# Loading the weights of a two-layer MoE trunk: 2 MB double pages, w_down by whole rows, three loads in flight

## The chip, the core and the metric

The kernel runs on one core of a Trainium2 chip. The metric is the time of one execution in microseconds (us) on the device. Engines: PE (matrix multiply), DVE (VectorE), ACT (ScalarE), POOL (GpSimd) and SP (SyncE, which here only issues transfers), and 16 DMA engines that move data between the main memory and the core's on-chip memory.

## What is computed

Two layers work on 512 tokens of width 1024 in fp32. Each layer has an input projection, a token mixer (a gated MLP in layer 0, a short convolution in layer 1), cross-attention to 256 memory rows, an output projection, a layer norm, and then 16 experts, of which each token uses two:

```python
for i in range(DEPTH):
    z = x @ w_in                       # 1024 x 1536 or 1024 x 2048
    tok, q = ...                       # token mixer; queries
    xa = memory_cross_attention(q, mem, w_kv[i])
    o = jnp.concatenate([tok, xa], axis=-1) @ w_out[i]
    x = layer_norm(ALPHA * x + o, ln1_g[i], ln1_b[i])
    # router: one of 4 groups, two experts in it
    for e in range(N_EXPERTS):         # 16
        h = jax.nn.silu(xt @ w_gate[e]) * (xt @ w_up[e])     # 1024 x 512 each
        out = out + combine[:, e:e + 1] * (h @ w_down[e])    # 512 x 1024
    x = layer_norm(ALPHA * x + f, ln2_g[i], ln2_b[i])
```

An expert's three matrices have 2 MB each. All weights together have 222 MB, of which the experts have 192, and each is used once.

## The kernel before, in words

**Arithmetic.** An fp32 product is made of three matmuls (`mm3`, L172 to 176): a number is split into a high part of reduced precision and a low part, the rest. A weight therefore passes two engines before PE: ACT copies `raw` to `high` (L144), DVE computes `low = raw - high` (L145). The three matmuls stand on L174 (high, high), L175 (low) and L176.

**Pages.** The on-chip memory is cut into 24 pages of 8 KB per partition, 1 MB each (`page`, `drop`, L64 to 74). Everything large lives in them: activations, raw weights, split weights. A page that is dropped goes to the end of a list; the next tile takes the first one of the list and must wait until the last reader of that page is done. All of this is decided when the program is built.

**The weight stream.** `Stream` (L96) has the weights in the order of their use, in units of 1 MB. `pump` splits what is loaded, up to `ahead` halves in front of PE (4, and 6 among the experts, where `whole` splits a page at once), and loads the next unit when more pages are free than `keep` and what the splits still want (L155). `fetch` (L118) issues a load on SP's queue; a load waits until the one `flight` places before it has landed: 2 at the start, 4 among the experts.

```python
            elif len(self.todo) > self.stop and len(free_pages) > self.keep + max(0, self.ahead - len(self.ready)):
                self.fetch()
```

Gate and up matrices are loaded by pairs of rows (`add_pairs`), a contiguous 4 KB per partition and row block. `w_down` and the projections are loaded by column halves (`add`), in runs of 2 KB. `moe_weights` (L906) orders the units of an expert: gate and up of rows 0 to 511, gate and up of rows 512 to 1023, then the two column halves of the expert before.

**The experts.** `experts` (L622) goes over 16 experts. POOL gathers up to 128 tokens of an expert, PE transposes them (`xtrans`), multiplies by gate and up (`gate_up`, accumulators `ga`, `ua`), ACT and DVE form `h`, PE transposes it (`htrans`, tile `ht`, one buffer). One expert later `down` (L674) multiplies by `w_down`, one column half after the other (accumulator `ya`), ACT scales each half on its way out (L686), and POOL adds the rows to `rd` in the main memory by a scatter. Near the end `W.keep` and `W.stop` (L710) hold loads back so that pages stay free for the rest of the layer; a last sum (`ra`) and the second layer norm follow.

**Order.** A scheduler in the build orders the instructions of each engine by a simulated timeline; on the chip each engine runs its list in that order. Before each layer's experts stands a branch on `nover` (L853, for experts with more than 128 tokens, not taken here), over which no instruction is moved. At the start, SP's queue holds `mem`, two loads of `w_kv`, `x`, and then, issued by `late_dma`, the router's weights and three loads for layer 0's gating unit (`sgu`, L251 to 256), ahead of the second two loads of `w_kv`.

Of the kernel before, what the change touches and what calls it, by code (L numbers as in the profile page):

```python
# [18 lines left out]
FT = mybir.dt.float32  # L19
# [8 lines left out]
P = 128  # L28
# [14 lines left out]
N_PAGES = 24  # L43
# [4 lines left out]
def trunk(ctx, tc, x, mem, w_in_a, sgu_ln_g, sgu_ln_b, sgu_w, sgu_b, w_in_b, conv_w, w_kv, w_out,  # L48
# [13 lines left out]
    uid = [0]  # L62

# [8 lines left out]
    def drop(*ts):  # L72
        for t in ts:
            free_pages.append(held.pop(id(t))[0])

# [19 lines left out]

    class Stream:  # L96
        def __init__(self):
            self.todo, self.raw, self.ready = [], [], []
# [4 lines left out]
        def add_pairs(self, w, k0):  # L103

            self.todo.append(bass.AP(tensor=w.tensor, offset=w.offset + k0 * 512,
                                     ap=[[2 * 512, P], [256 * 512, 2], [1, 2 * 512]]))

        def add_wide(self, w, k0):

            self.todo.append(bass.AP(tensor=w.tensor, offset=w.offset + k0 * D, ap=[[D, P], [P * D, 2], [1, D]]))  # L110

        def add(self, w, k0, n0):

            n = w.shape[1]
            self.todo.append(bass.AP(tensor=w.tensor, offset=w.offset + k0 * n + n0,
                                     ap=[[n, P], [P * n, 4], [1, 512]]))

        def fetch(self):  # L118
            self.sent += 1
            t = page("raw", [P, 4, 512])  # L120
            src = self.todo.pop(0)
            with ExitStack() if self.behind is None else tc.issue_after(self.behind):
                load = sp.dma_start(t if src.ap[-1][1] == 512 else t.rearrange("p (a b) n -> p a (b n)", a=2), src).ins
# [5 lines left out]
            self.raw.append([t, 0])  # L129

        def split(self):
            t, h = self.raw[0]
            if self.whole and not h:
                high, low = page("high", [P, 4, 512], FR), page("low", [P, 4, 512], FR)
                src = t
                self.ready += [Half(high[:, 0:2], low[:, 0:2]), Half(high[:, 2:4], low[:, 2:4], high, low)]
                self.raw[0][1] = 2
            else:
                g = page("split", [P, 2, 2, 512], FR)
                src, high, low = t[:, 2 * h:2 * h + 2], g[:, 0], g[:, 1]  # L140
                self.ready.append(Half(high, low, g))
                self.raw[0][1] += 1
# [4 lines left out]
            if self.raw[0][1] == 2:  # L147
                self.raw.pop(0)
                drop(t)

        def pump(self):
            while True:
                size = 2 if self.whole and self.raw and not self.raw[0][1] else 1
                if not self.hold and len(self.ready) + size <= self.ahead and self.raw and len(free_pages) >= size:
                    self.split()  # L155
                elif len(self.todo) > self.stop and len(free_pages) > self.keep + max(0, self.ahead - len(self.ready)):
                    self.fetch()
                else:
                    return
# [35 lines left out]

    def weights_kv(i):
        w = w_kv[i]
        for n in range(2):
            for k in range(2):
                W.add(w, k * 512, n * 512)  # L200

    def weights_cols(w, n):
        for k in range(2):
            W.add(w, k * 512, n * 512)

    def weights_out(i):
        w = w_out[i]
        for n in range(2):
            for k in (1, 0):
                W.add(w, k * 512, n * 512)  # L210
# [3 lines left out]
    W.fetch()  # L214
    W.fetch()
# [29 lines left out]
    def late_dma(dst, src):  # L245
        with tc.issue_after(xload.ins):
# [6 lines left out]
    sgu = page("sgu", [P, 4, H, P])  # L253
    sgw, sgb, sgt, cwr = sgu[:, 0], sgu[:, 1], sgu[:, 2], sgu[:12, 3, 0]
    late_dma(cwr, conv_w.rearrange("o t (b p) -> (o t b) p", p=P))
    cw = consts.tile([P, 3, 4], FT, name="cw")
    late_dma(sgw, bass.AP(tensor=sgu_w.tensor, offset=sgu_w.offset, ap=[[P, P], [P * P, H], [1, P]]))
    late_dma(sgb.rearrange("p h i -> p (h i)"),
                  bass.AP(tensor=sgu_b.tensor, offset=sgu_b.offset, ap=[[0, P], [1, H * P]]))

# [361 lines left out]
    def experts(i, lnp, fill, after, stop, fine=False):  # L622
# [72 lines left out]
        W.keep, W.flight = 5, 4  # L695
# [4 lines left out]
        for e in range(E):  # L700
# [205 lines left out]
    def moe_weights(i, first):  # L906
        def gu(e, k):
            W.add_pairs(w_gate[i, e], k * 512)
            W.add_pairs(w_up[i, e], k * 512)

        def dn(e):
            for n in range(2):
                W.add(w_down[i, e], 0, n * 512)
# [25 lines left out]
    W.keep = 8  # L939
# [9 lines left out]
    sg = page("sgln", [P, 2, MW])  # L949
    bcast_rows(sg[:, 0], sgu_ln_g[0])  # L950
    bcast_rows(sg[:, 1], sgu_ln_b[0])
# [9 lines left out]

    W.keep = 4
    a = project_t(xh, xl)
    qh, ql = page("qh", [P, H, S], FR), page("ql", [P, H, S], FR)
    for h in range(H):
        split_to(qh[:, h, :], ql[:, h, :], a[h])
    pr = softmax_scores(qh, ql, kt)
    drop(qh, ql, kt)
# [12 lines left out]
    W.keep = 5  # L981
# [18 lines left out]
    W.keep = 3  # L1000
# [79 lines left out]
    W.keep = 3  # L1080
# [37 lines left out]
```

## Time and profile before

| | |
|---|---|
| median of 3 runs | 1069.66 us (1065.61 to 1069.82) |
| the profiled execution | 1064.45 us, span of the profile 1062.8 us |
| PE busy | 989.5 us, 93% of the span |
| DVE busy, ACT busy | 779.6 us, 630.6 us |
| DMA | 273.31 MB, mean 257 GB/s |
| first transpose for the experts of layer 0, of layer 1 | 217.4 us, 730.1 us from the span's start |
| first of layer 0's last sums | 532.5 us |

The profile has the times of one execution. A busy time sums what an engine worked; for PE, whose matmuls overlap, it says little beyond whether there were gaps. The DMA share of a stretch is the mean busy share of the 16 DMA engines, near 1 (and slightly over, by overlap) when they are full. A wait names the engine that waited, the line that waited, and what released it.

### The profile page before, as it was taken

How to read it: one execution, taken by the hardware profiler on the slowest of the kernel's cores; microseconds unless marked ns; L12 is line 12 of the kernel's file. 1: busy time of each engine (PE TensorE's matmuls, PEld its weight loads, DVE VectorE, ACT ScalarE, POOL GpSimd, SP SyncE). 2: the span in 40 equal slices, each digit the busy share in tenths (PEclk: the TensorE clock that was granted, in tenths of full speed). 3: DMA queues.
4: the chain of work that ended last, by engine and by line, in shares of the span. 5: the costliest groups of instructions: out<-in, count | busy, mean ns of one | idle time of the engine just before them, and what ended most of it. 6: DMA issues, size and time to landing. Idle time of an engine off the chain costs nothing.

```text
span 1062.8 us, 12859 instructions
## 1 busy us (share of the span) xinstructions
PE 989.5 (93%) x4815; PEld 809.4 (76%) x4816; DVE 779.6 (73%) x880; ACT 630.6 (59%) x684; POOL 177.1 (17%) x115
## 2 busy tenths in 40 slices
PE   8999999789999988999999999987899999988995
PEld 6788889668888876777678887875788888866863
DVE  4648657869898677878794656575799898768875
ACT  4536524458888667668553524234778887667762
POOL 0000014312212202001100000223053212220113
PEclk9999999979999999999999999987899999999998
DMA  9713449459999999979671424491699999999833
GB/s 327 269 41 119 156 162 319 160 195 360 358 370 371 367 349 365 336 274 321 200 280 40 159 79 152 146 401 45 210 355 362 372 361 360 347 359 336 282 68 154
DMA packets 102220, 273.31 MB, mean 257 GB/s; under 512 B 10442, under 2 KB 10966, under 8 KB 102152
## 3 DMA queue, kind: packets, MB, share of 16 engines
q1 hardware_dynamic: 89480, 242.84, 62.9%
q0 software_dynamic: 11808, 26.97, 9.2%
q10 hardware_dynamic: 864, 2.62, 0.7%
q8 instruction: 39, 0.64, 0.2%
q14 instruction: 29, 0.24, 0.1%
HBM read 262.22 MB, written 26.21 MB: 271 GB/s over the span
## 4 chain that ended last, share of the span: by engine, by line
PE 61%; DVE 8%; ACT 4%; DMA 4%; issue 2%; DVEq 0%; ACTq 0%; POOLq 0%; SPq 0%
PE ua L175 5%; PE ua L176 5%; PE ya L175 5%; PE ya L174 5%; PE ua L174 5%; PE ya L176 5%; PE ga L175 5%; PE ga L174 4%; PE ga L176 4%; DVE low L145 4%; ACT high L144 3%; PE xt L648 2%; PE za L176 2%; PE za L174 2%; PE za L175 2%; DMA raw<-in_w_up_dram 2%
## 5 line engine op out<-in xcount | busy, mean ns | idle before, releaser
L145 DVE TENSOR_TENSOR low<-raw,high 128x2048 fp32r<-128x2048 f32 x189 | 428.7, 2288 | 78.8 <-ACT high L144 73.0
L144 ACT ACTIVATE high<-raw 128x2048 fp32r<-128x2048 f32 x189 | 357.9, 1914 | 54.5 <-PE ga L175 20.1
L175 PE MATMUL ua<-low,xgt 128*128 128x512 f32 x248 | 98.6, 397 | 16.7 <-DVE low L145 16.6
L144 ACT ACTIVATE split<-raw 128x1024 fp32r<-128x1024 f32 x66 | 68.5, 1058 | 76.7 <-PE za L176 26.1
L174 PE MATMUL ya<-high,ht 128*128 128x512 f32 x256 | 103.9, 407 | 2.5 <-ACT high L144 2.5
L176 PE MATMUL ya<-high,ht 128*128 128x512 f32 x256 | 101.5, 398 | 2.5 <-DVE ht L180 2.5
L175 PE MATMUL ya<-low,ht 128*128 128x512 f32 x256 | 102.6, 401 | 0.7 <-DVE low L145 0.7
L174 PE MATMUL ga<-high,xgt 128*128 128x512 f32 x248 | 98.9, 399 | 3.0 <-ACT high L144 3.0
L175 PE MATMUL ga<-low,xgt 128*128 128x512 f32 x248 | 98.7, 398 | 2.1 <-DVE low L145 1.9
L174 PE MATMUL ua<-high,xgt 128*128 128x512 f32 x248 | 98.1, 395 | 0.2
L176 PE MATMUL ga<-high,xgt 128*128 128x512 f32 x248 | 97.6, 393 | 0.0
L176 PE MATMUL ua<-high,xgt 128*128 128x512 f32 x248 | 97.0, 391 | 0.0
L145 DVE TENSOR_TENSOR split<-raw,split 128x1024 fp32r<-128x1024 f32 x57 | 68.6, 1220 | 38.5 <-ACT split L144 37.8
L639 POOL DMA_INDIRECT xg<-x1d,idxs x32 | 50.3, 1572 | 248.7 <-PE xt L648 238.6
L175 PEld LDWEIGHTS ua<-low,xgt 128*128 128x128 f32 x248 | 46.6, 188 | 30.8 <-DVE low L145 21.6
L145 POOL TENSOR_TENSOR split<-raw,split 128x1024 fp32r<-128x1024 f32 x9 | 21.5, 2390 | 283.2 <-DVE sto L446 146.9
L174 PE MATMUL za<-xh,split 128*128 128x512 f32 x160 | 61.7, 392 | 2.0 <-ACT xh L179 2.0
L635 POOL DMA_INDIRECT rd<-h,idxs x16 | 41.4, 2589 | 127.0 <-ACT h L686 126.4
L175 PE MATMUL za<-xl,split 128*128 128x512 f32 x160 | 62.5, 391 | 0.0
L176 PE MATMUL za<-xh,split 128*128 128x512 f32 x160 | 61.5, 390 | 0.0
L174 PEld LDWEIGHTS ya<-high,ht 128*128 128x128 f32 x256 | 48.8, 191 | 14.3 <-ACT high L144 3.0
L176 PEld LDWEIGHTS ya<-high,ht 128*128 128x128 f32 x256 | 48.4, 189 | 14.6 <-DVE ht L180 3.4
(250 smaller groups left out, 1893.9 us busy)
## 6 DMA issues: line engine op xcount, KB each, us to landing
raw<-in_w_gate_dram SPq DMA_DIRECT2D x64, 1024.0 KB, 10.3
raw<-in_w_up_dram SPq DMA_DIRECT2D x64, 1024.0 KB, 10.1
raw<-in_w_down_dram SPq DMA_DIRECT2D x64, 1024.0 KB, 10.5
raw<-in_w_kv_dram SPq DMA_DIRECT2D x8, 1024.0 KB, 7.3
raw<-in_w_out_dram SPq DMA_DIRECT2D x8, 1024.0 KB, 5.1
raw<-in_w_in_b_dram SPq DMA_DIRECT2D x8, 1024.0 KB, 10.7
raw<-in_w_in_a_dram SPq DMA_DIRECT2D x6, 1024.0 KB, 5.5
x1d<-x POOLq DMA_DIRECT2D x8, 512.0 KB, 5.8
```

Source lines behind the costliest of these rows:

```text
L144: act.activation(high, src, AF.Copy)
L145: (pool_e if self.on_pool(self.count) else vec).tensor_tensor(low, src, high, op=OP.subtract)
L174: pe.matmul(o, a[0], b[0], start=start, stop=False)
L175: pe.matmul(o, a[0], b[1], start=False, stop=False)
L176: return pe.matmul(o, a[1], b[0], start=False, stop=stop)
L635: added[e] = pool_e.indirect_dma_start(out=rd[i], out_offset=bass.IndirectOffsetOnAxis(ap=tabs[e][0], axis=0), in_=ys[e % 2], in_offset=No ...
L639: pool_e.indirect_dma_start(out=xg[:, e % 2], out_offset=None, in_=x1d[i], in_offset=bass.IndirectOffsetOnAxis(ap=tabs[e][0], axis=0), bou ...
L648: pe.transpose(t[:, k, :], xg[:, e % 2, k0:k0 + 2 * P - 1:2], ident)
```

## The change

There are now 20 single pages and two double pages of 2 MB. A unit of the stream is a whole matrix or a 512-column block of one, of 2 MB: if a double page is free when its turn comes, one load fetches it all; if not, it comes as two loads of 1 MB to two single pages. A double page is free again when both its halves are split. `w_down` is loaded by whole rows (4 KB runs) instead of column halves, except for the last expert of each layer, and `down` then has both column halves in two accumulators at once and evicts both at the end. Three loads are in flight among the experts. Several `keep` numbers change, and the gating unit's three loads and small transposes move behind the attention scores of layer 0.

```diff
-N_PAGES = 24
+N_PAGES = 20
+N_DOUBLES = 2
...
+    def double():
+        i = free_doubles.pop(0)
+        uid[0] += 1
+        return i, pages.tile([P, 8, 512], FT, name=f"raw_{uid[0]}", tag=f"db{i}", bufs=1)
...
+        def pairs(self, w):
+
+            ap = lambda k, n: bass.AP(tensor=w.tensor, offset=w.offset + k * 512, ap=[[2 * 512, P], [256 * 512, n], [1, 2 * 512]])
+            return self.add([ap(0, 2), ap(512, 2)], ap(0, 4))
+
+        def rows(self, w):
+
+            ap = lambda k, n: bass.AP(tensor=w.tensor, offset=w.offset + k * D, ap=[[D, P], [P * D, n], [1, D]])
+            return self.add([ap(0, 2), ap(256, 2)], ap(0, 4))
...
+        def fetch(self, single=False):
+            self.sent += 1
+            u = self.todo.pop(0)
+            if u.whole is not None and free_doubles and not single:
+                u.at, t = double()
+                self.load(t, u.whole)
+                u.raw = [t[:, 0:4], t[:, 4:8]]
+            else:
+                for src in u.parts:
+                    t = page("raw", [P, 4, 512])
+                    self.load(t, src)
+                    u.raw.append(t)
+            u.left = len(u.parts)
...
+            if self.half == 2:
+                self.half = 0
+                self.plan.pop(0)
+                u.left -= 1
+                if u.at is None:
+                    drop(t)
+                elif not u.left:
+                    free_doubles.append(u.at)
+
+        def room(self):
+            if not self.todo or len(self.todo) <= self.stop:
+                return False
+            u = self.todo[0]
+            if u.whole is not None and free_doubles:
+                return True
+            return len(free_pages) >= len(u.parts) + self.keep + max(0, self.ahead - len(self.ready))
...
         def down(e, evict):
+            if e < last:
+                a = [acc("ya") for _ in range(2)]
+                for k in range(4):
+                    g = W.next()
+                    for n in range(2):
+                        mm3(a[n], (ht[:, 0, k, :], ht[:, 1, k, :]), (g[:, 0, n, :], g[:, 1, n, :]), k == 0, k == 3)
+                    W.done(g)
+                for n in range(2):
+                    evict(n, a[n])
+                return
...
-        W.keep, W.flight = 5, 4
+        W.keep, W.flight = 5, 3
...
-                W.stop = stop - 2 if stop else 0
+                W.stop = stop - 1 if stop else 0
...
         first()
         for e in range(E):
-            gu(e, 0)
+            g, u = W.pairs(w_gate[i, e]), W.pairs(w_up[i, e])
+            d = W.rows(w_down[i, e - 1]) if e else None
+            W.use((g, 0), (u, 0))
             if e == E - 1:
-                dn(e - 1)
-            gu(e, 1)
+                W.use((d, 0), (d, 1))
+            W.use((g, 1), (u, 1))
             if 0 < e < E - 1:
-                dn(e - 1)
-        dn(E - 1)
+                W.use((d, 0), (d, 1))
+        w = w_down[i, E - 1]
+        for n in range(2):
+            u = W.add([bass.AP(tensor=w.tensor, offset=w.offset + n * 512, ap=[[D, P], [P * D, 4], [1, 512]])])
+            W.use((u, 0))
...
-    W.keep = 8
+    W.keep = 10
...
-                W.keep, W.ahead = (2, 3) if i == 0 else (1, 2)
+                W.keep, W.ahead = (3, 3) if i == 0 else (2, 2)
```

The scheduler's order changes with it at many places. Three of them bear on the prediction. The first is SP's queue at the start (`raw` is a weight, `sgu` the gating unit's page). Before:

```order
L213 DMA mem_75<-in_mem_dram 128x2x1024
L123 DMA raw_77<-in_w_kv_dram 128x4x512
L123 DMA raw_79<-in_w_kv_dram 128x4x512
L217 DMA x_73<-in_x_dram 128x1024 x2
L217 DMA x_74<-in_x_dram 128x1024 x2
L247 DMA rw<-in_router_w_dram 128x8x16
L247 DMA rb<-in_router_b_dram 128x16
L247 DMA sgu_108<-in_conv_w_dram 12x128
L247 DMA sgu_108<-in_sgu_w_dram 128x4x128
L247 DMA sgu_108<-in_sgu_b_dram 128x512
L123 DMA raw_85<-in_w_kv_dram 128x4x512
L123 DMA raw_187<-in_w_kv_dram 128x4x512
```

Now, from the router's weights on:

```order
L291 DMA rw<-in_router_w_dram 128x8x16
L291 DMA rb<-in_router_b_dram 128x16
L144 DMA raw_85<-in_w_kv_dram 128x8x512
L144 DMA raw_182<-in_w_in_a_dram 128x8x512
L144 DMA raw_184<-in_w_in_a_dram 128x4x512
L144 DMA raw_186<-in_w_in_a_dram 128x4x512
L144 DMA raw_302<-in_w_in_a_dram 128x8x512
L144 DMA raw_374<-in_w_out_dram 128x8x512
L291 DMA sgu_713<-in_conv_w_dram 12x128
```

The second pair of `w_kv` loads is one load of 2 MB, and the gating unit's loads stand behind the input projection's.

The second place is SP's queue in the late part of layer 0's experts. Before, each expert has six loads of 1 MB:

```order
L123 DMA raw_3338<-in_w_gate_dram 128x2x1024
L123 DMA raw_3356<-in_w_up_dram 128x2x1024
L123 DMA raw_3374<-in_w_gate_dram 128x2x1024
L123 DMA raw_3412<-in_w_up_dram 128x2x1024
L123 DMA raw_3432<-in_w_down_dram 128x4x512
L123 DMA raw_3463<-in_w_down_dram 128x4x512
```

Now, for two experts (`128x4x1024` is a whole matrix of 2 MB in a double page):

```order
L144 DMA raw_3451<-in_w_gate_dram 128x2x1024
L144 DMA raw_3453<-in_w_gate_dram 128x2x1024
L144 DMA raw_3524<-in_w_up_dram 128x4x1024
L144 DMA raw_3556<-in_w_down_dram 128x4x1024
L144 DMA raw_3590<-in_w_gate_dram 128x2x1024
L144 DMA raw_3592<-in_w_gate_dram 128x2x1024
L144 DMA raw_3663<-in_w_up_dram 128x2x1024
L144 DMA raw_3665<-in_w_up_dram 128x2x1024
L144 DMA raw_3697<-in_w_down_dram 128x4x1024
```

The whole gate now comes ahead of the whole up, and the second and third matrix in a row find a double page or not by turns.

The third place is ACT's list in the same part: `high` is a split's first half, `ht` the copy of the transposed `h`, `h<-ya` or `y<-ya` an eviction, `h<-ga` the SiLU. Before, from one `ht` to the SiLU:

```order
L179 ACTIVATE ht<-htr 128x512
L686 ACTIVATE y_170<-ya,gates 128x512
L144 ACTIVATE high_3837<-raw_3642 128x2048
L144 ACTIVATE high_3857<-raw_3660 128x2048
L144 ACTIVATE high_3888<-raw_3698 128x2048
L179 ACTIVATE xgt_1693<-xt 128x512
L144 ACTIVATE high_3904<-raw_3718 128x2048
L664 ACTIVATE h_1692<-ga 128x512
```

Now, with the splits ahead of `ht` (`raw_3451` and `raw_3453` are the gate's two pages, `raw_3524` the up's double):

```order
L179 ACTIVATE high_3606<-raw_3451 128x2048
L228 ACTIVATE xgt_1677<-xt 128x512
L179 ACTIVATE high_3659<-raw_3453 128x2048
L732 ACTIVATE h_1676<-ya,gates 128x512 x2
L228 ACTIVATE ht<-htr 128x512
L179 ACTIVATE high_3643<-raw_3524 128x2048
L179 ACTIVATE high_3693<-raw_3524 128x2048
L700 ACTIVATE h_1676<-ga 128x512
```

Both evictions stand together, and two splits instead of four stand between `ht` and the SiLU.

## Rows read from the trace of the kernel before

**Rows 1.** The page: busy time of PE and the other engines; POOL's DMA queue (packets, MB).

```profile
PE 989.5 (93%) x4815; PEld 809.4 (76%) x4816; DVE 779.6 (73%) x880; ACT 630.6 (59%) x684; POOL 177.1 (17%) x115
...
q0 software_dynamic: 11808, 26.97, 9.2%
```

**Rows 2.** Busy time by stretch: engines, then granted clock, DMA share, GB/s.

```profile
260.00:372.00 112.00, 112.00 (x529) 93.00 (x528) 94.14 (x62) 87.38 (x75) 25.99 (x13) 1.00 1.02 367
372.00:462.00 90.00, 80.83 (x369) 63.78 (x367) 69.00 (x43) 59.69 (x51) 10.75 (x8) 1.00 1.01 353
462.00:470.00 8.00, 6.15 (x26) 4.37 (x25) 6.00 (x5) 6.55 (x5) 1.56 (x1) 1.00 0.38 75
...
920.00:1003.00 83.00, 75.61 (x345) 60.37 (x344) 64.84 (x41) 58.74 (x50) 9.88 (x6) 1.00 0.96 338
```

**Rows 3.** Timeline of SP, layer 0's experts: start, duration, the pairs of w_down loads.

```profile
266.20 3.17 SPq L123 DMA_DIRECT2D raw<-in_w_down_dram  x2
...
284.13 3.17 SPq L123 DMA_DIRECT2D raw<-in_w_down_dram  x2
...
415.84 4.80 SPq L123 DMA_DIRECT2D raw<-in_w_down_dram  x2
...
457.47 12.40 SPq L123 DMA_DIRECT2D raw<-in_w_down_dram  x2
```

**Rows 4.** Waits of PE, whole span: us in total, times, longest.

```profile
PE ua L175 <- DVE low L145: 16.6, 12, 1.8
...
PE ga L174 <- ACT high L144: 3.0, 1, 3.0
...
PE ya L174 <- ACT high L144: 2.5, 2, 1.3
...
PE za L174 <- ACT xh L179: 2.0, 1, 2.0
```

**Rows 5.** Timeline of all engines, 441 to 446 us, behind one expert's down matmuls.

```profile
441.05 0.60 ACT L179 ACTIVATE ht<-htr 128x512 fp32r<-128x512 f32 x1 [2.01 <-PE ya L175]
...
442.12 5.51 ACT L144 ACTIVATE high<-raw 128x2048 fp32r<-128x2048 f32 x3
...
443.86 0.40 PE L176 MATMUL ga<-high,xgt 128*128 128x512 f32 x1
444.06 2.29 DVE L145 TENSOR_TENSOR low<-raw,high 128x2048 fp32r<-128x2048 f32 x1 [1.69 <-ACT high L144]
...
444.10 0.48 PE L174 MATMUL ua<-high,xgt 128*128 128x512 f32 x1
```

**Rows 6.** Busy time by stretch: one of 2 KB runs, two of 4 KB, one mixed.

```profile
27.00:36.00 9.00, 9.00 (x45) 7.46 (x44) 8.81 (x10) 6.67 (x8) 0.00 (x0) 1.00 1.01 372
415.80:419.40 3.60, 3.44 (x21) 2.77 (x20) 2.77 (x2) 2.35 (x2) 1.03 (x1) 1.00 1.00 394
453.00:457.00 4.00, 4.00 (x19) 3.26 (x18) 2.15 (x4) 2.40 (x2) 0.00 (x0) 1.00 1.04 372
15.00:18.00 3.00, 3.00 (x27) 3.00 (x26) 0.00 (x0) 0.00 (x0) 0.00 (x0) 1.00 1.12 253
```

**Rows 7.** DMA issues: count, KB each, us to landing.

```profile
x1d<-x POOLq DMA_DIRECT2D x8, 512.0 KB, 5.8
rd<-x POOLq DMA_DIRECT2D x8, 512.0 KB, 8.8
```

**Rows 8.** Waits of SP's queue, 372 to 480 us.

```profile
SPq L123 <- DVE low L145: 24.9, 8, 11.6
```

**Rows 9.** Timeline of SP at the start.

```profile
8.84 4.31 SPq L247 DMA_DIRECT2D sgu<-in_conv_w_dram  x1
...
14.40 1.91 SPq L123 DMA_DIRECT2D raw<-in_w_kv_dram  x2
```

**Rows 10.** Timeline of SP, end of layer 0: the reload of x.

```profile
520.91 1.01 SPq L728 DMA_DIRECT2D x<-rd  x2
```

**Rows 11.** The chain that ended last, 515 to 545 us: the first of the last sums.

```profile
532.53 0.86 PE ra L745 x2
```

More of the change, by code (lines that the diff above doesn't have):

```diff
@@ L62, in trunk @@
     uid = [0]
+    free_doubles = list(range(N_DOUBLES))
     def page(name, shape, dtype=FT):
@@ L101, in __init__, with columns, add, use @@
             self.after, self.behind, self.loads, self.flight = None, None, [], 2
[L103 to L112, printed above, removed]
-            n = w.shape[1]
[L115 to L121, printed above, removed]
+        def columns(self, w, n0):
+            n = w.shape[1]
+            return self.add([bass.AP(tensor=w.tensor, offset=w.offset + k * 512 * n + n0, ap=[[n, P], [P * n, 4], [1, 512]])
+                             for k in range(2)],
+                            bass.AP(tensor=w.tensor, offset=w.offset + n0, ap=[[n, P], [P * n, 8], [1, 512]]))
+        def pairs(self, w):
[4 more added lines that the diff above has]
+            return self.add([ap(0, 2), ap(256, 2)], ap(0, 4))
+        def add(self, parts, whole=None):
+            u = Unit(parts, whole)
+            self.todo.append(u)
+            return u
+        def use(self, *parts):
+            self.plan += parts
+        def load(self, t, src):
+            n = t.shape[1]
             with ExitStack() if self.behind is None else tc.issue_after(self.behind):
-                load = sp.dma_start(t if src.ap[-1][1] == 512 else t.rearrange("p (a b) n -> p a (b n)", a=2), src).ins
+                load = sp.dma_start(t if src.ap[-1][1] == 512 else t.rearrange("p (a b) n -> p a (b n)", b=2), src).ins
             self.loads.append(load)
@@ L146, in split @@
             self.count += 1
-            if self.raw[0][1] == 2:
-                self.raw.pop(0)
-                drop(t)
+            if self.half == 2:
[13 more added lines that the diff above has]
+            return len(free_pages) >= len(u.parts) + self.keep + max(0, self.ahead - len(self.ready))
         def pump(self):
             while True:
-                size = 2 if self.whole and self.raw and not self.raw[0][1] else 1
-                if not self.hold and len(self.ready) + size <= self.ahead and self.raw and len(free_pages) >= size:
+                size = 2 if self.whole and not self.half else 1
+                if (not self.hold and len(self.ready) + size <= self.ahead and self.plan and self.plan[0][0].raw
+                        and len(free_pages) >= size):
                     self.split()
-                elif len(self.todo) > self.stop and len(free_pages) > self.keep + max(0, self.ahead - len(self.ready)):
+                elif self.room():
                     self.fetch()
@@ L948, in trunk @@
             keep_warm(4)
-    sg = page("sgln", [P, 2, MW])
-    bcast_rows(sg[:, 0], sgu_ln_g[0])
-    bcast_rows(sg[:, 1], sgu_ln_b[0])
+    W.keep = 6
+    a = project_t(xh, xl)
+    qh, ql = page("qh", [P, H, S], FR), page("ql", [P, H, S], FR)
+    for h in range(H):
+        split_to(qh[:, h, :], ql[:, h, :], a[h])
+    pr = softmax_scores(qh, ql, kt)
+    drop(qh, ql, kt)
+    sgu = page("sgu", [P, 4, H, P])
+    sgw, sgb, sgt, cwr = sgu[:, 0], sgu[:, 1], sgu[:, 2], sgu[:12, 3, 0]
+    late_dma(cwr, conv_w.rearrange("o t (b p) -> (o t b) p", p=P))
+    cw = consts.tile([P, 3, 4], FT, name="cw")
+    late_dma(sgw, bass.AP(tensor=sgu_w.tensor, offset=sgu_w.offset, ap=[[P, P], [P * P, H], [1, P]]))
+    late_dma(sgb.rearrange("p h i -> p (h i)"),
+                  bass.AP(tensor=sgu_b.tensor, offset=sgu_b.offset, ap=[[0, P], [1, H * P]]))
     t = bank([P, 12], "cwt")
@@ L960, in trunk @@
     vec.memset(sgt[64:P, :, 0:64], 0.0)
[L962 to L968, printed above, removed]
     W.keep = 3
@@ L980, in trunk @@
     drop(*xh, *xl)
-    W.keep = 5
+    W.keep = 6
+    sg = page("sgln", [P, 2, MW])
+    bcast_rows(sg[:, 0], sgu_ln_g[0])
+    bcast_rows(sg[:, 1], sgu_ln_b[0])
     for c in range(NC):
@@ L999, in trunk @@
     lnp = ln_params(ln1_g[0], ln1_b[0])
-    W.keep = 3
+    W.keep = 5
     def mixer_end(i, ch, cl, lnp):
@@ L1079, in trunk @@
     lnp = ln_params(ln1_g[1], ln1_b[1])
-    W.keep = 3
+    W.keep = 5
     mixer_end(1, ch, cl, lnp)
```

43 lines of the change are left out of this document (14 added, 29 removed).

## The prediction, made before the changed kernel was run

> **What bounds the kernel now.** I read the engine totals first: PE is busy for 93% of the span [rows 1], but that is an average over stages. The table by stretch splits one expert stage. From 260 to 372 us PE has no idle time and the DMA share is 1.02; from 372 to 462 PE is busy for 80.83 of 90 us with the DMA still at 1.01; from 462 to 470 the DMA falls to 0.38 [rows 2]. Layer 1 ends alike: 7.4 us of 83 lost from 920 to 1003. So an expert stage begins bound by PE, living off weights loaded ahead, and ends short of weights. The loads show the pace: from one pair of w_down loads to the next 17.93 us early (266.20 to 284.13), and late (415.84 to 457.47, two experts) 20.8 us each [rows 3].
>
> What PE waits for is in the waits: 16.6 us in 12 waits of an up matmul for the low half of a split, 3.0 us for a high half at the start of layer 1's experts, 2.5 us in two waits of a down matmul: 22.1 us in all [rows 4]. That is about all that a better supply of weights can give back in the expert stages; matmuls, splits and bytes stay as many as they were.
>
> Two causes stand behind those waits at once. One is the DMA, which is full. The other is ScalarE's fixed order: the copy into ht waits 2.01 us for the down matmuls (the tile has one buffer), an eviction follows, and only then three splits without a gap, from 442.12 on. PE needs the first of them at 444.10; VectorE can begin its low half only at 444.06, and that takes 2.29 [rows 5]. Three splits without a gap mean that their pages had landed: part of the wait is order, not supply.
>
> **The change, part by part.** *Packets.* 30 of the 32 w_down matrices now come in rows of 4 KB, not 2 KB. In a stretch that loads only 2 KB rows the DMA moved 372 GB/s at full share, in two with 4 KB rows alone 394 and 372 [rows 6]; by length these give 382. One w_down is 2.10 MB: 5.65 us becomes 5.50, so 0.15 us per expert, with 0 and 0.33 as bounds. The DMA is full for some 13 experts of each layer: 2 x 13 x 0.15 = **-3.9 us** (0 to -8.6). [...]
>
> *Larger loads.* By SyncE's order 52 of 170 weight loads are of 2 MB: 104 of 222 MB, so rather under half than "most", because there are two double pages and a unit that finds none goes as two singles. Four loads in flight of 1 MB become three of 1 or 2 MB. With the DMA share already at 1.01 there is no gap for them to close [rows 2]: 0.
>
> *ScalarE's order.* Late in the stage both gate pages are now split ahead of ht, and both up pages come right behind it. PE then has 24 gate matmuls before it needs an up page, where it had 12; at 0.24 us each [rows 5] that is 5.8 us instead of 2.9. Against that, both column halves of w_down end together, so two evictions may stand before the split instead of one. Copy and eviction took 1.1 us (441.05 to 442.12), the split 1.9 and 2.3: 5.3 from the end of the down matmuls, and 5.9 with one eviction more. So the wait shrinks from the 2 us seen to about 0.1 to 0.4, by four fifths. But supply caps what that is worth. An expert needs six loads, 6.29 MB, and its gathers and scatters at most 0.58 MB (queue 0's 26.97 MB [rows 1] less 16 copies of 512 KB [rows 7], over 32 experts): 6.87 MB at 353 GB/s is 19.5 us, against 20.8. So 1.3 us per late expert is order, and four fifths of it 1.04. There are nine such experts (five from 372 to 478, four from 920 to 1003, at 20.8 us each): **-9.4 us** (0 to -11.7).
>
> *The hole.* The second w_down load of the pair at 457.47 takes SyncE until 469.9, and the DMA is idle meanwhile [rows 2, 3]; it waits 11.6 us for a split to free a page [rows 8]. A free double is now taken without regard to the pages kept back, which should shorten this. Behind it PE loses one wait of 1.3 us [rows 4]: **-1.3 us** (0 to -1.3).
>
> *Two megabytes less ahead.* At layer 1's branch on `nover` 16 MB of expert weights stand before it in SyncE's order, where there were 18; layer 0 has 12 in both. Two MB at 338 GB/s [rows 2] are 6.2 us, paid in full if supply sets the end of the stage, not at all if PE does. I take half: **+3 us** (0 to +6.2).
>
> *Doubles held whole.* The first half of a 2 MB load can be split only when the second has landed, 1.05 MB at 353 GB/s or 3.0 us later, and its page comes free only when both are used. About 1.5 doubles per expert over nine late experts are 13 such delays, 0 to +40 us. Since both gate pages are split ahead, most are covered; I take **+2 us**.
>
> *Start.* Three small loads for the gating unit no longer stand ahead of the second pair of key and value weights. SyncE sat on the first for 4.31 us and issued the pair only at 14.40 [rows 9]; the DMA ran at 253 GB/s from 15 to 18 [rows 6], which against 394 loses 1.1 us of loading. PE waits 2.0 us for the last x copy before the query projection [rows 4], which comes late since transposes of x stand behind value matmuls; 28 of 32 now stand ahead of them. **-2 us** (+1, a split of VectorE more in front, to -3.1, both effects in full). The small loads return behind the scores, where PE has matmuls of the next projection to run; they cost nothing there, and up to the 4.31 us that SyncE sat on the first if PE should come to wait for them.
>
> *Scatter.* The last scatter before each final sum starts up to one eviction, 0.6 us, later. The reload of x behind it is issued at 520.91 and the first sum comes at 532.53 [rows 10, 11]; these 11.6 us cover it: 0, or +1.2 uncovered in both layers.
>
> The sum: -3.9 - 9.4 - 1.3 + 3 + 2 - 2 = **-11.6 us**. Against the profiled execution, 1064.45 us (span 1062.8), that is 1052.9. Its time lies 5.2 us under the median of the three runs, 1069.66; against that the forecast is **1058 us**.
>
> **The rivals.** *Supply recovered whole.* The 22.1 us of waits and the start's 3.1 all go: 1044.5. For it: the waits repeat at one place of the order, which changes. Against: the DMA is full where they stand. I count anything below 1050 here.
>
> *No change.* The rate at which weights arrive is capped, whatever the rows' length, and the order's gain meets the same full DMA: hole and start, -3.3, and two MB less, +3, leave 1069.4. Averages of 353 to 367 GB/s over long stretches speak for it [rows 2], 394 GB/s in a short one against [rows 6]. [...]
>
> *Slower: doubles starve PE late.* Where the lead is under the 2 MB of a double, PE waits for its second half. At 3.0 us for 13 doubles, half of them uncovered, 20 us are lost instead of 2, and the splits behind them come in bursts that ScalarE serves in order, so the order's 9.4 us go too: 1058 + 18 + 9.4 = 1085.4. It decides as soon as the six halves split ahead run empty before a double lands. For it: the lead is gone at 372 us already. Against: about 4 MB stay in flight, and a full DMA is a matter of throughput, not of delay.
>
> *It does less than it says.* Half the weights keep 1 MB loads; were the doubles at work in the mixers alone, packets and start would remain, -5.9: 1063.8. The order shows 42 of 52 doubles on expert weights, so I give it nothing of its own.
>
> **How the numbers follow.** About 0.5%, 5.3 us, is what a measurement of this kernel can tell from no change. The forecast's own case (1050 to 1064) has 0.45, supply recovered whole 0.14, no change (1064 to 1075) 0.22, slower 0.19. So faster 0.59, same 0.22, slower 0.19. The range leaves out one in ten on each side: from 1043, the whole recovery with packets at their bound, to 1077, where a third of the late doubles are uncovered. The own case spans the bounds of packets and order.
>
> **What would show it.** Right: late experts 19.5 to 20 us apart; PE's waits for low halves under 8 us in all; no idle 8 us of DMA near 465; half as many packets for w_down; the query projection about 2 us earlier. Wrong: waits of ScalarE or PE for loads of up and gate of 3 us at a time, a short supply that begins before 372, or a layer 1 that loses what layer 0 gains.

## The result and the profile after

The changed kernel takes **1082.49 us** (median of 4 runs, 1081.92 to 1083.89) where the kernel before, run beside it, takes 1069.53. The ratio is 1.0138, 95% interval 1.0117 to 1.016: slower by 1.4%, outside the range of the prediction and on the other side. The medians are 13.0 us apart; the two profiled executions, 1081.92 and 1064.45, are 17.5, as that of the kernel before was a quick one.

The page of the changed kernel, first its engines and queues, then the chain that ended last:

```profile
span 1080.2 us, 12566 instructions
PE 1002.1 (93%) x4815; PEld 818.4 (76%) x4816; DVE 774.4 (72%) x880; ACT 626.9 (58%) x686; POOL 180.2 (17%) x115
...
q1 hardware_dynamic: 73288, 242.84, 60.5%
q0 software_dynamic: 11808, 26.97, 9.0%
...
issue 15%; DMA 7%; POOL 3%; DVE 1%; PE 1%; POOLq 0%; DVEq 0%; SPq 0%
DMA rd<-h,idxs 5%; DMA rd<-y,idxs 2%; POOL rd L671 1%; POOL xg L675 1%; PE ra L791 1%; DMA x<-rd 0%; DVE x L817 0%; DVE st L804 0%; DVE x L835 0%; PE ra L792 0%; PE ra L793 0%; DVEq L1162 0%; DVE mv L808 0%; DVE ve L810 0%; POOLq L671 0%
```

The same two lines of the kernel before, its loads and its chain:

```profile
q1 hardware_dynamic: 89480, 242.84, 62.9%
...
PE 61%; DVE 8%; ACT 4%; DMA 4%; issue 2%; DVEq 0%; ACTq 0%; POOLq 0%; SPq 0%
```

PE's share is 93% as in [rows 1], and the bytes are the same, in fewer packets: the totals do not say where 17 us went. The chain points at one place: before, it ran through PE's matmuls, and now it runs through the scatter into rd, which the prediction had costed at nothing. It is only a pointer, as the shares that it names add up to 27% of the span. PE's waits over the whole span (us in total, times, longest), against [rows 4]:

```profile
PE ra L791 <- DMA x<-rd: 8.8, 2, 5.0
PE ga L223 <- ACT high L179: 8.2, 2, 5.3
...
PE ya L224 <- DVE low L180: 4.8, 4, 1.6
...
PE ua L224 <- DVE low L180: 3.3, 3, 1.8
...
PE ga L224 <- DVE low L180: 2.5, 2, 1.5
```

The 16.6 us of up matmuls waiting for low halves are down to 3.3. In their place stand 8.2 us in two waits of a gate matmul for a high half, 4.8 us of down matmuls and 2.5 of gate matmuls for low halves, 18.8 us in all, and a wait that the kernel before did not have, 8.8 us in front of the last sums for the reload of x. The stretches of [rows 2], in the changed kernel (engines, clock, DMA share, GB/s):

```profile
260.00:372.00 112.00, 111.35 (x525) 91.84 (x523) 91.24 (x60) 85.07 (x73) 28.95 (x14) 1.00 0.99 361
372.00:462.00 90.00, 83.64 (x373) 67.80 (x374) 71.08 (x45) 64.46 (x54) 13.82 (x8) 0.96 0.98 346
462.00:470.00 8.00, 8.00 (x40) 6.59 (x39) 8.00 (x6) 5.76 (x7) 0.48 (x1) 1.00 0.86 328
920.00:1003.00 83.00, 75.13 (x335) 61.07 (x334) 63.24 (x40) 56.45 (x48) 12.70 (x7) 0.96 0.92 333
```

The hole from 462 to 470 is closed (75 to 328 GB/s). But PE works little more than before in the late stretches, 83.64 of 90 us for 80.83, 75.13 of 83 for 75.61, and the granted clock, 1.00 there before, is 0.96.

**Where the 17.4 us of span are lost**, by the first and last matmuls of each stage in the two traces: the scores of layer 0 start 2.8 us earlier (61.40 for 64.22 us); the output projection starts 5.7 later (131.9 for 126.2), so 8.5 are lost between; the first transpose for layer 0's experts comes 8.7 later (226.1 for 217.4), 3.0 more; layer 0 from there to the end of its last sums loses 0.9, the second mixer 0.7, and layer 1 from its first transpose to the end of the span 7.1 (339.8 for 332.7). Two places hold most of it.

The first place, on VectorE and on ScalarE's queue:

```profile
107.33 0.37 ACTq L301 DMA_DIRECT2D sgln<-in_sgu_ln_g_dram  x1
...
110.84 1.42 DVE L470 SCALAR_TENSOR_TENSOR v<-v,mv,sgln 128x512 f32<-128x512 f32 x2 [11.90 <-DMA sgln<-in_sgu_ln_g_dram]
```

The gain and bias of the gating unit's layer norm (tile sgln) are asked for at 107.33 us; before, ScalarE's queue asked for them at 32.94, right behind the transposes of x. The diff, in lines not printed above, moves the three lines that ask for them from ahead of the query projection to behind the projection of u. VectorE stands still for 11.90 us, and the norms, the splits of the attention weights and the attention behind them all come late.

The second place, the last scatter of layer 1 (POOL), the reload of x (SP), and the first sum (PE); the changed kernel, then the kernel before:

```profile
1043.21 1.55 POOL L671 DMA_INDIRECT rd<-h,idxs  x1 [16.43 <-ACT h L732]
...
1049.87 2.77 SPq L774 DMA_DIRECT2D x<-rd  x4
...
1054.60 2.08 PE L791 MATMUL ra<-x,ident 128*128 128x512 f32 x2 [5.00 <-DMA x<-rd]
```

```profile
1026.23 1.88 POOL L635 DMA_INDIRECT rd<-h,idxs  x1 [11.97 <-ACT h L686]
...
1032.94 2.45 SPq L728 DMA_DIRECT2D x<-rd  x4
```

The scatter comes 17.0 us later in a layer that began 10.3 later. The change loads the last expert's gate and up as whole matrices, and w_down of the expert before (expert 14) behind all four halves; before, it stood between the first two and the last two. The order of use in the diff still has expert 14's down between the halves, but in the instruction order that came of it, its 24 matmuls run behind the last gate and up matmuls (1036.3 to 1042.2 us; the last gate matmul ends at 1031.7). Before, they ran ahead of the last 24 of those (1019.6 to 1025.2; the last gate matmul ended at 1028.0). So the eviction, scatter and reload, 11.4 us from scatter to sum, no longer lie beside the gate and up matmuls of expert 15.

### The profile page after: what moved, and what is told of

The parts are those of the page before. It is cut to its first block, busy times and chain, and to the rows that moved or that the text cites. A ratio compares the mean times of both kernels' runs of the same rounds, so it can differ in the third digit from the quotient of the medians.

```text
span 1080.2 us, 12566 instructions
## 1 busy us (share of the span) xinstructions
PE 1002.1 (93%) x4815; PEld 818.4 (76%) x4816; DVE 774.4 (72%) x880; ACT 626.9 (58%) x686; POOL 180.2 (17%) x115
## 3 DMA queue, kind: packets, MB, share of 16 engines
q1 hardware_dynamic: 73288, 242.84, 60.5%
## 5 line engine op out<-in xcount | busy, mean ns | idle before, releaser
L225 PE MATMUL ya<-high,ht 128*128 128x512 f32 x256 | 101.5, 399 | 0.0
L675 POOL DMA_INDIRECT xg<-x1d,idxs x32 | 59.4, 1856 | 250.4 <-PE xt L684 237.7
L223 PE MATMUL ya<-high,ht 128*128 128x512 f32 x256 | 97.6, 403 | 0.0
L224 PEld LDWEIGHTS ya<-low,ht 128*128 128x128 f32 x256 | 48.4, 189 | 17.3 <-DVE low L180 6.5
L223 PEld LDWEIGHTS ga<-high,xgt 128*128 128x128 f32 x248 | 47.4, 191 | 18.4 <-ACT high L179 8.8
L228 ACT ACTIVATE xgt<-xt 128x512 fp32r<-128x512 f32 x64 | 37.1, 593 | 37.7 <-PE ua L224 26.2
## 6 DMA issues: line engine op xcount, KB each, us to landing
raw<-in_w_up_dram SPq DMA_DIRECT2D x13, 2048.0 KB, 11.6
```

The costliest lines, as they stand in the source:

```text
L223: pe.matmul(o, a[0], b[0], start=start, stop=False)
L224: pe.matmul(o, a[0], b[1], start=False, stop=False)
L225: return pe.matmul(o, a[1], b[0], start=False, stop=stop)
L228: r = act.activation(hi, src, AF.Copy)
L675: pool_e.indirect_dma_start(out=xg[:, e % 2], out_offset=None, in_=x1d[i], in_offset=bass.IndirectOffsetOnAxis(ap=tabs[e][0], axis=0), bou ...
```

## The experiments

**Theory A**: those two moved orders cost the time. **Theory B**: the 2 MB doubles with three loads in flight starve the engines. The first four kernels undo or do one part each. A ± behind a difference of two ratios joins the halves of their 95% intervals, as the root of the sum of squares.

**Norm parameters early.** The changed kernel, with

```
     drop(qh, ql, kt)
+    sg = page("sgln", [P, 2, MW])
+    bcast_rows(sg[:, 0], sgu_ln_g[0])
+    bcast_rows(sg[:, 1], sgu_ln_b[0])
     sgu = page("sgu", [P, 4, H, P])
```

and the same three lines taken out behind the projection of u. They do not go back to their old place, ahead of the query projection, but right behind the scores.

> The changed kernel with one thing undone: the gain and bias of the gating unit's layer norm (tile sgln) are loaded right behind the scores again, ahead of the two next projections, not behind the projection of u. Theory A (two moved orders cost the time: this load, and the last w_down behind a whole gate and up): VectorE's 11.9 us wait for sgln is gone, the first output matmul of layer 0 comes at about 123 to 125 us instead of 131.9, and the median falls by 7 to 9 us, to about 1074 to 1075. Theory B (the 2 MB doubles with three loads in flight starve the engines, in the expert stages above all): the first output matmul comes earlier too, but the weights it then needs come no sooner; the time gained is waited off in front of layer 0's experts and the median stays above 1080.

Measured: 1074.66 us, ratio to the kernel before 1.0052 (1.0033 to 1.0072), where the changed kernel had 1.0138. The output projection starts at 125.1 us, 6.8 earlier. VectorE begins the norm 17.9 us sooner than in the changed kernel, without a wait:

```profile
92.98 0.74 DVE L470 SCALAR_TENSOR_TENSOR v<-v,mv,sgln 128x512 f32<-128x512 f32 x1
```

The three moved lines cost 0.86% of 1067 us: 9.2 ± 3.1 us. PE still waits 8.8 us for the reload of x.

**The last expert's loads in the old order.** The changed kernel, with

```
+            if e == E - 1:
...
+                g, u = W.add([ap(w_gate[i, e], 0)]), W.add([ap(w_up[i, e], 0)])
+                d = W.rows(w_down[i, e - 1])
+                W.use((g, 0), (u, 0), (d, 0), (d, 1))
+                g, u = W.add([ap(w_gate[i, e], 512 * 512)]), W.add([ap(w_up[i, e], 512 * 512)])
+                W.use((g, 0), (u, 0))
+                break
```

> The changed kernel with one thing undone: in each layer the last expert's gate and up come as four loads of 1 MB again, with w_down of the expert before between the first two and the last two, so that it is not loaded behind all of them. Theory A: the last scatter but one of layer 1 starts about 10 us earlier against the end of the gate and up matmuls, PE's 8.8 us of waits for the reloaded x are gone, and the median falls by 5 to 9 us, to about 1074 to 1078. Theory B: the last w_down still comes late, since the doubles ahead of it hold the pages; less than 2 us, about 1081.

Measured: 1071.69 us, ratio 1.004 (1.0024 to 1.0056): 0.98%, or 10.5 ± 2.9 us, under the changed kernel, somewhat more than theory A expected. The last scatter, 13.4 us sooner in a layer that begins 5.8 sooner:

```profile
1029.81 1.55 POOL L671 DMA_INDIRECT rd<-h,idxs  x1 [10.64 <-ACT h L732]
...
1036.13 3.15 SPq L774 DMA_DIRECT2D x<-rd  x4
...
1044.57 1.02 PE L791 MATMUL ra<-x,ident 128*128 128x512 f32 x2
```

The first sum no longer waits for x. From the first transpose to the end of the sums, layer 0 is 6.2 us shorter than in the changed kernel (322.3 for 328.5); layer 1, counted to the end of the span, is 6.8 shorter (333.0 for 339.8). The edit also brings that one expert's gate and up back as four loads of 1 MB, with up's first half ahead of gate's second; what part of the 10.5 us is the place of w_down alone was not measured.

**Both.**

> Both of the orders undone in one kernel. Theory A: the two add up, 13 to 17 us under the changed kernel: 1065 to 1070, level with the kernel before or a little under it. Theory B: 1077 to 1081, well over the kernel before.

Measured: 1064.94 us, ratio **0.9963** (0.9946 to 0.998). The parts add up: 1.0138 less 0.9963 is 1.75%, 18.7 ± 2.9 us, against 9.2 + 10.5. By the medians alone the three are 17.6, 7.8 and 10.8 us. What is left of the change is worth 0.4%, 3.9 ± 1.8 us. Theory B, which wanted 1077 or more here, falls.

**Rows alone.** The kernel before, with 15 of 16 w_down matrices of each layer by whole rows, and down() of the changed kernel for them:

```
-                W.add(w_down[i, e], 0, n * 512)
+                if e < E - 1:
+                    W.add_wide(w_down[i, e], n * 256)
+                else:
+                    W.add(w_down[i, e], 0, n * 512)
```

> The kernel before with one part of the change alone: 15 of 16 w_down matrices of each layer are loaded by whole rows, in two loads of 256 rows, and their column halves computed together, as in the changed kernel. No doubles, 24 pages, four loads in flight, and all loads in the old order. The prediction's terms for packets and for ScalarE's order, -3.9 and up to -9.4, give 1056 to 1066 if they hold without the doubles. Theory B says that only the doubles cost, so it too expects 1062 to 1066. If rows and halves together are worth nothing by themselves: 1068 to 1071.

Measured: 1065.78 us, ratio 0.9992 (0.9964 to 1.002). Rows and halves together are worth 1 ± 3 us. Gate and up keep their old order here, first halves ahead of second halves, so this kernel does not test the prediction's term for ScalarE's order, which went by the whole gate ahead of the whole up. Its waits of PE and its late stretches:

```profile
PE ua L175 <- DVE low L145: 20.5, 13, 1.8
```

```profile
260.00:372.00 112.00, 112.00 (x529) 92.97 (x528) 94.05 (x62) 87.53 (x75) 25.61 (x13) 1.00 1.00 367
372.00:462.00 90.00, 81.16 (x377) 65.45 (x375) 68.89 (x45) 61.59 (x54) 12.04 (x9) 1.00 0.98 353
```

367 and 353 GB/s, to the digit those of [rows 2], at a DMA share 0.02 to 0.03 lower: in these stretches longer rows kept the DMA engines a little less busy and brought no byte sooner.

**Columns again**, the converse: the kernel with both orders undone, w_down by column halves in two loads, computed one after the other.

```
-            if e < last:
+            if False:
...
-            d = W.rows(w_down[i, e - 1]) if e else None
+            d = W.halves(w_down[i, e - 1]) if e else None
```

> The kernel with both orders undone, with w_down again in two loads by column halves (rows of 2 KB) that are computed one after the other; gate and up keep their doubles. The prediction's terms for packets and ScalarE's order would come back here, 10 to 13 us: 1075 to 1078. If rows and halves are worth as little as the rows-only kernel says (0.9992 of the kernel before): 1064 to 1068.

Measured: 1066.2 us, ratio 0.999 (0.9977 to 1.0002), against 0.9963 with rows: 2.9 ± 2.3 us, not 10 to 13. Here too gate and up keep their order, now the new one, so this measures rows and halves, and not that order.

**More in flight.** Two kernels: the rows-only one with six loads of 1 MB in flight (`W.keep, W.flight = 5, 6`), and the one with both orders undone with four instead of three.

> The rows-only kernel with six loads of 1 MB in flight instead of four. It moved 350 to 374 GB/s from 260 to 460 us at a DMA share of 0.98 to 1.01. If that is a cap, the same rates and 1064 to 1067. If it is what four loads in flight can ask for: 380 GB/s or more in that stretch, late experts 1 us closer together, and 1056 to 1061.

> The kernel with both orders undone, with four loads in flight instead of three. If three loads, some of them of 2 MB, leave gaps in the DMA (share 0.95 to 0.98 from 780 to 940 us, where the kernel before had 0.99 to 1.03), a fourth closes them: 2 to 5 us less, 1060 to 1063. If the DMA is capped whatever is in flight: 1064 to 1066.

Measured: 1068.0 us, ratio 1.0015 (0.9994 to 1.0036), and 1066.53 us, 0.9985 (0.997 to 1). Neither is faster than the kernel it was made from (0.9992 and 0.9963). With six in flight the DMA moved

```profile
260.00:372.00 112.00, 112.00 (x529) 93.01 (x528) 96.25 (x61) 86.94 (x74) 24.54 (x12) 1.00 1.02 371
372.00:462.00 90.00, 82.89 (x387) 67.24 (x385) 70.56 (x46) 65.80 (x56) 15.36 (x10) 1.00 1.00 356
```

1% more than [rows 2]. What that won came back at the end of layer 1: its last gate matmul ends 4.1 us sooner than in the rows-only kernel (1021.4 for 1025.5), its first sum comes 1.9 later (1039.0 for 1037.1), after 5.8 us of waiting for the reload of x. In these two stretches the rate is between 344 and 371 GB/s in six kernels (before, changed, both orders, rows alone, six in flight, no doubles), with three, four or six loads in flight. But 371 is no ceiling: in the kernel before, ahead of layer 1's experts, weight loads and copies to the main memory together reached

```profile
691.00:718.00 27.00, 22.19 (x143) 20.09 (x141) 19.88 (x50) 8.98 (x16) 6.11 (x8) 0.81 1.02 404
```

Why these two stretches, in which rows are gathered and scattered too, stay below these 404 GB/s at a DMA share of 0.97 to 1.02 is not shown.

**No doubles.** Both orders undone, `N_PAGES = 24`, `N_DOUBLES = 0`.

> The kernel with both orders undone, but no double pages: 24 single pages instead of 20 and two doubles, so every weight comes in loads of 1 MB, in the same order and with three in flight. From 230 to 260 us that kernel moved 263 GB/s where the kernel before moved 339: 2.3 MB of lead less at the start of layer 0's experts, 6.4 us at 355 GB/s if it is paid in full. Theory C (the doubles cost lead, since a page of 1 MB is refilled sooner than a double): 330 to 340 GB/s in that stretch, layer 0's stage as short or shorter, and a median 2 to 7 us under 1064.9. Theory D (the doubles are worth their pages: the loads they save make up for the lead): 1065 to 1070. Theory E (size of the loads makes no difference, the bytes in flight and the cap of the DMA do): within 2 us of 1064.9, with 3 MB in flight instead of up to 6.

Measured: 1066.88 us, ratio 0.9986 (0.9973 to 0.9999), 2.5 ± 2.3 us over the kernel with doubles. The lead is there, 323 GB/s from 230 to 260 us for 263, and so is a late stage at a granted clock of 1.00 (372 to 462 and 920 to 1003 us, where the kernel with doubles has 0.96). In the two traces layer 1 is 7.3 us shorter without doubles, from its first transpose to its first sum (305.0 for 312.3), and the first transpose comes 1.1 us later, layer 0 to the end of its sums takes 3.2 us more and the second mixer 2.9, so the spans end alike (1063.4 and 1063.6). Theory C falls; between D and E its time does not decide. The gain at the start is gone, though: the scores begin at 63.9 us.

**The start.** Two kernels ask where its 2.8 us come from: the rows-only kernel with the small gating loads behind the scores (and sgln in front of them), and the kernel with both orders undone with `W.fetch(True)` for the second half of the first key and value weights, so that this one comes as two loads of 1 MB.

> The kernel before with w_down by whole rows (as in the rows-only kernel, 1065.8) and the start of the changed kernel: the gating unit's small loads behind the scores, with the gain and bias of its layer norm right in front of them. If the start's gain is that of the changed kernel, the scores begin 2 to 3 us earlier (about 61.5 instead of 64.2 us) and the median is 1062 to 1064. If it is waited off before layer 0's experts, as routing and the values of layer 1 stand in the way there: 1065 to 1066.

> The kernel with both orders undone, with one load changed: the second half of the first key and value weights comes as two loads of 1 MB instead of one of 2 MB. The small gating loads stay behind the scores. The prediction gave the start's gain to the small loads out of the way; then the scores still begin at 61.5 to 62 us. If the gain comes from the double, which lands late as a whole, so that VectorE splits x ahead of it and PE transposes x instead of waiting, the scores begin at about 64 us, 2 us later, and the median is 0 to 3 us up.

Measured: 1066.83 us, ratio 0.9991 (0.9975 to 1.0007), and 1063.85 us, **0.9956** (0.9933 to 0.9979). The first score of the kernel before, of the changed one, and of these two:

```profile
64.22 0.28 PE L174 MATMUL sc<-kt,qh 128*128 128x256 f32 x1
```

```profile
61.40 0.28 PE L223 MATMUL sc<-kt,qh 128*128 128x256 f32 x1
```

```profile
64.07 0.28 PE L174 MATMUL sc<-kt,qh 128*128 128x256 f32 x1
```

```profile
60.78 0.28 PE L223 MATMUL sc<-kt,qh 128*128 128x256 f32 x1
```

Neither the small loads nor the key and value double alone is the reason. All kernels with a 2 MB load among the first weights begin the scores at 60.8 to 61.9 us, those without one at 63.9 to 66.4. A double moves the order in which VectorE takes the halves of x among the weight splits; that this order is the cause is likely, not shown.

**One double.** Both orders undone, `N_PAGES = 22`, `N_DOUBLES = 1`; and the same with the numbers of pages kept back at the mixer ends as before.

> The kernel with both orders undone, with 22 single pages and one double instead of 20 and two. Theory F (the routing of layer 0 loses time for want of pages: layer 1's value weights have no page to be split into until the route page is dropped, and the values end 12 to 14 us behind the count of tokens instead of before it): with two pages more the values end nearer to the count, the first gathered token is transposed 2 to 4 us sooner against the start, and the median is 1061 to 1064, since the first double still delays the splits of the second key and value weights behind those of x. Theory E (the DMA's cap decides in the expert stages): the time gained before the stage is only lead, 1064 to 1067.

> The kernel with 22 pages and one double, and with the numbers of pages kept back at the two mixer ends as in the kernel before (3 and 2 for 5 and 3 in layer 0, 3 and 1 for 5 and 2 in layer 1). Theory F: more loads and splits ahead of the first expert of each layer, 1060 to 1063. Theory E: within 1.5 us of the one-double kernel.

Measured: 1069.78 us, ratio 1.0019 (1.0006 to 1.0032), and 1072.16 us, 1.0038 (1.0022 to 1.0054). By their medians both are slower than any of their theories allowed. Half of theory F held: with two pages more the values of layer 1 end ahead of the count of tokens again (209.2 and 210.7 us; with two doubles 213.4 and 199.2), and the experts begin at 218.1 for 220.5. But the expert stage itself then takes 325.5 us to the end of its last sum, for 320.2, and the kernel with one double is 0.6% slower than the one with two. Why one double serves that stage worse than two or none stays open.

## Why the prediction was wrong

The forecast was 11.6 us less, and 1.4% more came, 13 us by the medians and 14.8 by the ratio. Two costs that it had at nothing, in *Start* and in *Scatter*, make up 18.7 ± 2.9 us. Without them the change is worth 3.9 ± 1.8 us, a third of the forecast; most of what is missing there is *ScalarE's order*.

**The step that failed first: *Start*.** It looked at three small loads that leave the front, and let them "cost nothing" behind the scores. It did not see that the diff moves a fourth thing, the sgln loads, behind the projection of u on ScalarE's queue, with a norm on VectorE right behind them: +9.2 us, by the run that asks for them behind the scores. In the same step the size of the gain was right, -2 against -2.8 us, by luck: in the rows-only kernel with the small loads out of the way, the query projection came 1.6 us sooner (38.59 for 40.14), but the scores only 0.15 (64.07).

**The step that failed second: *Scatter*.** "One eviction, 0.6 us, later" was the cost of computing both column halves together; that was not what moved the scatter. The loads of the last expert put its whole gate and up ahead of expert 14's w_down, expert 14's down matmuls fell behind them, and the cover that the step counted on [rows 10, 11] was gone: +10.5 us, by the run with the old order (and four loads of 1 MB for that expert).

***ScalarE's order*, -9.4, was mis-sized.** Its first half came true: waits of up matmuls for low halves fell from 16.6 to 3.3 us. The time did not follow. The nearest pair is the kernel without doubles and the rows-only kernel with the changed start: both have 24 pages, loads of 1 MB, rows, and the small loads behind the scores. The first has the whole gate ahead of the whole up (and three loads in flight, and other `keep` numbers), and its up matmuls wait 4.5 us for low halves, where the second's wait 15.2:

```profile
PE ua L224 <- DVE low L180: 4.5, 3, 1.8
```

```profile
PE ua L175 <- DVE low L145: 15.2, 10, 1.8
```

Their times differ by 0.5 ± 2.2 us (0.9986 and 0.9991). Nor did the late experts clearly come closer together, as the prediction said they would. From expert 8 to expert 14 of layer 0, changed kernel against before, the transposes of h are 19.5 us apart for 20.6, (500.5 - 383.8)/6 and (497.1 - 373.6)/6, the SiLUs 19.8 for 20.5, the copies into ht 20.5 in both. From the first transpose of h to the last, layer 0 takes 280.6 us for 281.8 and layer 1 280.6 for 285.0: 5.6 us, against 9.6 for all terms of the expert stages together (with the hole and the two lead terms). Two things stand against the term.

First, its 1.3 us per late expert does not come out of its own rows: 353 GB/s [rows 2] over 20.8 us are 7.34 MB, not the 6.87 counted, and the DMA share was 1.01 all the while, so there was no idle transfer time for an earlier split to use. The 0.24 us per gate matmul is one gap in [rows 5]; 529 matmuls in 112 us [rows 2] are 0.21 us each, so 24 of them cover 5.1 us and not 5.8. Second, the wait for ScalarE's order did not all end, some of it moved. ScalarE in the changed kernel, layer 1, and PE's gate matmul behind it:

```profile
976.16 0.60 ACT L228 ACTIVATE xgt<-xt 128x512 fp32r<-128x512 f32 x1 [4.97 <-PE ua L224]
...
979.32 0.59 ACT L228 ACTIVATE ht<-htr 128x512 fp32r<-128x512 f32 x1
979.79 10.90 ACT L179 ACTIVATE high<-raw 128x2048 fp32r<-128x2048 f32 x6
```

```profile
985.35 0.79 PE L223 MATMUL ga<-high,xgt 128*128 128x512 f32 x1 [5.27 <-ACT high L179]
```

This is the picture of [rows 5] with six splits behind ht in place of three. A gate matmul is what waits now, for the third of the six, 5.27 us in one piece, where the kernel before had waits of 1.8 at most in its late stretches. It is order and not supply: by the semaphore that the third split waits for, its load had landed at 971.5 us, while ScalarE stood still for 4.97 us behind a copy that waited for PE.

***Packets*, -3.9, is not decided.** Rows and halves by themselves measured 1 ± 3 us in one kernel and 2.9 ± 2.3 in the other, and the packets fell as foretold (73288 for 89480); the rates of the rows-only kernel, 367 and 353 GB/s as before, speak against a gain.

***The hole***: closed, as foretold; the DMA moves 328 GB/s there. What that was worth was not measured by itself. ***Two megabytes less ahead*** and ***Doubles held whole***, +3 and +2: with the orders undone, the kernel with doubles is 2.5 ± 2.3 us quicker than the one without, so the rival that made them the cause, with nearly the measured time (1085.4), had the wrong mechanism. What layer 1 loses with the doubles in the two traces, 7.3 us, the stages before it give back.

**A cost that no step had: from the output projection to the experts.** With both orders undone this takes 95.0 us (125.5 to 220.5) where the kernel before takes 91.2 (126.2 to 217.4), and of the start's gain nothing reaches the experts. With 20 pages the values of layer 1 run behind the count of tokens and not before it, as their weights find no page to be split into. That pages are the cause is argued, not shown: with 24 pages and no doubles the values again end before the count, and this way still takes 93.4 us (128.2 to 221.5).

Of the signs named, the query projection came 0.7 us early, not 2, and waits for low halves came to some 11 us (4.8, 3.3 and 2.5), not under 8. Packets and the DMA near 465 came as foretold. The last sign of the wrong case, "a layer 1 that loses what layer 0 gains", shows once both orders are undone: layer 0, from its first transpose to the end of its sums, is 7.5 us shorter than before (320.2 for 327.6), and layer 1, from its first transpose to the end of the span, 2.7 longer (335.4 for 332.7). The fastest kernel here is the one with both orders undone and the start in single loads: 0.9956 of the kernel before, 0.4% less, just under what the prediction called measurable, and not to be told from the one with both orders undone alone (0.9963).

## What to carry to other kernels

Go through a diff line by line for every load that changes its place, the small ones above all, and ask of each which engine consumes it next: here three lines for 4 KB of parameters cost 9.2 us, as much as the largest term of this prediction hoped to gain. Where loads are regrouped, look at the last round by itself; here its order put a scatter and a reload beside other work, and the larger unit took that away. And where a stretch shows a full DMA, multiply its rate by the time you hope to shorten before you count on a wait removed from an engine there: in this kernel such waits came back at other places, one of them as 5.27 us in one piece.

## What the hardware showed that was not expected

One wait inside a full stage cost, by an estimate, more than its length. Around the wait of 5.27 us the granted clock of the changed kernel was (stretches as above):

```profile
977.50:984.70 7.20, 2.59 (x18) 2.12 (x16) 3.84 (x4) 6.66 (x6) 1.58 (x1) 1.00 1.00 364
984.70:991.50 6.80, 6.15 (x15) 4.80 (x16) 6.80 (x4) 6.00 (x4) 0.00 (x0) 0.50 0.58 187
991.50:998.00 6.50, 6.50 (x30) 5.37 (x29) 2.75 (x2) 1.70 (x1) 0.00 (x0) 1.00 0.95 345
```

PE worked 2.59 of 7.2 us, then ran 6.8 us at a granted clock of 0.50, with 15 matmuls in 6.15 us where the next stretch has 30 in 6.50: by that, an estimate, 2.9 us on top of the 5.3. In the kernel before PE was idle for 9.2 of the 90 us from 372 to 462, in pieces of at most 1.8 us [rows 4], and the clock stayed at 1.00 [rows 2]. But in these traces the length of a wait alone does not tell whether the clock falls. In the rows-only kernel a wait of 1.78 us ended at 953.7 us, and the clock was 0.50 behind it as well:

```profile
950.00:955.00 5.00, 3.21 (x15) 2.30 (x14) 3.62 (x2) 4.95 (x3) 1.81 (x2) 1.00 1.03 407
955.00:958.40 3.40, 3.40 (x10) 2.62 (x9) 3.40 (x3) 1.02 (x2) 0.00 (x0) 0.50 1.05 325
```
